# A hybrid diffusion trunk on one core: adaLN chunks moved between stages, a residual's split reordered, one more unnormed tile, an early chunk one pass later

## The chip, the core and the metric

The kernel runs on one core of a Trainium2 chip, as one program for the whole inference step. The metric is the device time of one execution in microseconds (us). A core's engines each work through their own queue in the order in which the program was written: TensorE (PE, with its weight loads as PEld), VectorE (DVE), ScalarE (ACT), GpSimd (POOL, next to idle here) and SyncE (SP, which issues the DMAs). They wait for each other through semaphores.

## The reference

Four layers on 384 tokens of width 1024 (128 context tokens, 256 latent tokens). The token mixer of layer i has kind i mod 3, and a ConvFFN follows each:

```python
for i in range(DEPTH):                       # 4
    kind, j = i % 3, i // 3
    sh1, sc1, gt1, sh2, sc2, gt2 = ada_params(cond, w_ada[i], b_ada[i])   # silu(cond) @ w_ada + b
    h = rms_norm(x, g_mix[i]) * (1 + sc1) + sh1
    if kind == 0:   y = chunk_gmlp(h, ...)   # u, v = split(gelu(h @ w_in)); (u * spatial(rms_norm(v))) @ w_out
    elif kind == 1: y = multi_pool(h, ...)   # centred mean over 2, 4, 8, 16 tokens minus h, grouped product
    else:           y = attention(h, ...)    # windowed, grouped queries, sinks
    x = x + gt1 * y
    h = rms_norm(x, g_ffn[i]) * (1 + sc2) + sh2
    a, u = split(h @ w_ffn_in[i])
    x = x + gt2 * ((gelu(depthwise_conv3(a)) * u) @ w_ffn_out[i])
```

All is float32. Outputs: x of both token groups, and the new keys and values.

## The kernel before, in words

x lies transposed in SBUF as 8 row tiles d = 0 to 7 of 128 x 384 (features on partitions, tokens along the row; 0 to 127 have the context's adaLN values, 128 to 383 the latent's, hence two column ranges, GRPS).

**Products.** A float32 product is made of three passes in fp32r: each operand is split into hi and lo, and wh\*rh + wl\*rh + wh\*rl are summed in PSUM (`mm3`, L688). Weights come in chunks of 128 x 1024 floats (512 KB) in one fixed order, `chunk_plan`. SP loads them into five buffers (`load`, L330); `w_split` has ACT copy a chunk to whi (L349) and DVE subtract to wlo (L356), some chunks ahead of PE (`w_get`).

**adaLN.** The 6 x 8 column groups of `w_ada` of each layer are chunks in the same stream, placed by the table ADA into stages ("gu", "go", "fi", "fo"; `weave` spreads them among a stage's weight chunks). An "ad" chunk is two DVE products with a sum (`ada_dve`, L391), taken in the stream's order behind the split of the weight chunk ahead of it. An "ap" chunk is four small matmuls (`ada_pe`, L409). The first two groups of layer 0 are "a0" chunks, on PE too (`a0_mm`, L1550; `a0_fin`, L1564).

**Residual and the next stage's input.** `out_proj` makes the eight d in five steps m: pairs (0,1), (2,3), (4,5), then 6 and 7 alone. After a step, `residual` updates x of each d on DVE (L464, two ranges), and `after(d)` of `prep` makes the *unnormed* input of the next stage, x times the gain A, split: on ACT hi = A\*x, two ranges (L624), on DVE lo = A\*x - hi, two ranges (L626), on ACT the square of x (L477), on DVE its sum (L479). For the pool's output `second` does the x update (L1057). Ahead of the pool, `extra` adds a bias to x on ACT (L1655). The ffn's `add_square` (L484) adds the last square, and `stats` (L536) then sums over features on PE.

**ffn.** Two column tiles (f = 0, 1) and those below NR = 3 are computed from the unnormed input and normed afterwards, with tile-wise products (L714, L719); meanwhile `norming` makes the normed input (`put_one`, L585 to L598), which the other 19 tiles of 22 use. "fr" and "fi" name chunks of the ffn's first product, "fo" of its second, "go" of the gMLP's output, "o" of the attention's. Stage names below are with the layer: go0, fo0, fi1, fo1.

**Start.** Layer 0's first product goes through k = 0 to 7 in `vmm` (three passes p of 6 matmuls); behind pass 0 `hook(k)` finishes the adaLN of k + 1 and has PE do the a0 chunks of k + 2.

## Time and profile before

| | |
|---|---|
| median of 3 runs | 1789.51 us (1787.81 to 1791.0) |
| the profiled execution | 1788.39 us, span 1786.6 us |
| granted TensorE clock, mean | 0.996 |
| PE busy | 1754.6 us (98%), 10230 matmuls |
| PEld busy | 1675.2 us (94%) |
| DVE busy | 1371.8 us (77%), 2369 instructions |
| ACT busy | 872.2 us (49%), 1635 instructions |
| weight DMAs, share of the 16 DMA engines | 50.9%, HBM 173 GB/s |
| chain that ended last, by engine | PE 61%, DVE 22%, ACT 8%, issue 5%, DMA 4% |

PE's busy share says little, since matmuls are pipelined and their ends modelled: what counts are the few places where PE waits, and who ends those waits. DVE's 77% is a mean over stages, some of which it fills.

### The profile page before, as it was taken

The numbers are of one execution on the slowest core, as the hardware profiler recorded it, in microseconds if no ns is written. First come the engines' busy times: TensorE is split into PE (matmuls) and PEld (weight loads), VectorE is DVE, ScalarE is ACT, GpSimd is POOL, SyncE is SP. The second block draws the span as 40 slices with busy tenths as digits, with TensorE's granted clock in tenths as the row PEclk, the third lists the DMA queues.
The fourth block names the chain that finished last, engine by engine and source line by source line (L and its number), as shares of the span: only waits on it lengthen the run. The fifth ranks groups of instructions, "written<-read, shape, count | busy, mean of one in ns | idle before, by whom it ended". The sixth has DMA issues, their size and how long they took to land.

```text
span 1786.6 us, 26835 instructions
## 1 busy us (share of the span) xinstructions
PE 1754.6 (98%) x10230; PEld 1675.2 (94%) x10230; DVE 1371.8 (77%) x2369; ACT 872.2 (49%) x1635; POOL 1.8 (0%) x30
## 2 busy tenths in 40 slices
PE   9999989999999999999998999999999999999999
PEld 7799889999998899998777999999988999999999
DVE  5888688888986888899687788887775767876632
ACT  3644236545455654432469565453454434755521
POOL 0000000000000000000000000000000000000000
PEclk9999999999999999999999999999999999999999
DMA  8764663555663355567550335655546344354341
GB/s 323 280 222 147 234 211 130 189 191 198 219 212 106 126 181 200 200 214 241 203 183 1 131 130 188 197 176 202 193 150 204 112 145 145 123 175 151 136 150 57
DMA packets 87636, 311.64 MB, mean 174 GB/s; under 512 B 10450, under 2 KB 10962, under 8 KB 87252
## 3 DMA queue, kind: packets, MB, share of 16 engines
q1 hardware_dynamic: 87220, 309.92, 50.9%
q8 instruction: 80, 1.31, 0.3%
q14 instruction: 48, 0.39, 0.1%
q10 hardware_dynamic: 288, 0.01, 0.0%
HBM read 308.06 MB, written 1.84 MB: 173 GB/s over the span
## 4 chain that ended last, share of the span: by engine, by line
PE 61%; DVE 22%; ACT 8%; issue 5%; DMA 4%; SPq 0%; DVEq 0%; ACTq 0%
PE mm L688 45%; DVE wlo L356 7%; DVE junk L391 7%; PE mm L862 6%; DMA wraw<-wts 4%; ACT whi L349 3%; DVE ct L736 3%; PE S L688 1%; PE mm L906 1%; ACT gg L745 1%; DVE gl L606 1%; PE adaT L688 1%; PE S L1138 1%; PE adaT L862 1%; PE psa L862 1%
## 5 line engine op out<-in xcount | busy, mean ns | idle before, releaser
L688 PE MATMUL mm<-hb,whi 128*128 128x384 f32 (+1 forms) x4064 | 888.7, 338 | 6.6 <-ACT whi L349 2.6
L688 PEld LDWEIGHTS mm<-hb,whi 128*128 128x128 f32 x4064 | 722.7, 189 | 11.6 <-ACT whi L349 3.3
L356 DVE TENSOR_TENSOR wlo<-wraw,whi 128x1024 fp32r<-128x1024 f32 (+2 forms) x390 | 466.3, 1201 | 213.7 <-ACT whi L349 212.4
L349 ACT ACTIVATE whi<-wraw 128x1024 fp32r<-128x1024 f32 (+2 forms) x390 | 399.3, 1034 | 270.3 <-PE mm L688 139.4
L688 PE MATMUL mm<-hb,wlo 128*128 128x384 f32 (+1 forms) x2032 | 521.4, 337 | 0.8 <-DVE wlo L356 0.8
L391 DVE SCALAR_TENSOR_TENSOR junk<-wraw,condb 128x1024 bf16<-128x1024 f32 x304 | 371.6, 1222 | 9.1 <-ACT condb L1618 2.7
L688 PEld LDWEIGHTS mm<-hb,wlo 128*128 128x128 f32 x2032 | 369.1, 189 | 1.3 <-DVE wlo L356 1.3
L745 ACT ACTIVATE gg<-ct 128x128 f32<-128x128 f32 (+1 forms) x152 | 47.0, 357 | 248.9 <-DVE ct L736 248.9
L688 PE MATMUL mm<-gh,whi 128*128 128x384 f32 x448 | 123.9, 338 | 3.2 <-ACT whi L349 3.2
L688 PE MATMUL mm<-gh,wlo 128*128 128x384 f32 x448 | 124.2, 338 | 2.4 <-DVE wlo L356 2.4
L688 PE MATMUL mm<-gl,whi 128*128 128x384 f32 x448 | 123.8, 338 | 0.0
L736 DVE SCALAR_TENSOR_TENSOR ct<-ab,par,ct 128x385 f32<-128x385 f32 x176 | 108.7, 619 | 6.4 <-ACT ct L734 2.7
L624 ACT ACTIVATE hb<-x,A 128x128 fp32r<-128x128 f32 x96 | 43.2, 457 | 103.9 <-DVE x L464 93.1
L862 PE MATMUL mm<-whi,hb 128*128 128x512 f32 x320 | 87.6, 399 | 0.0
L688 PEld LDWEIGHTS mm<-gh,whi 128*128 128x128 f32 x448 | 81.9, 189 | 4.1 <-ACT whi L349 4.1
L688 PEld LDWEIGHTS mm<-gh,wlo 128*128 128x128 f32 x448 | 82.0, 189 | 3.6 <-DVE wlo L356 3.6
L688 PEld LDWEIGHTS mm<-gl,whi 128*128 128x128 f32 x448 | 82.3, 189 | 0.0
L746 DVE TENSOR_TENSOR gg<-mm,gg 128x384 f32<-128x384 f32 x76 | 42.4, 558 | 47.4 <-ACT gg L745 46.7
L862 PEld LDWEIGHTS mm<-whi,hb 128*128 128x128 f32 x320 | 60.8, 190 | 15.6 <-ACT hb L573 0.4
L734 ACT ACTIVATE ct<-ab,par 128x385 f32<-128x385 f32 x88 | 62.7, 713 | 3.4
L464 DVE SCALAR_TENSOR_TENSOR x<-mm,prm,x 128x128 f32<-128x128 f32 x92 | 33.6, 411 | 22.9 <-PE mm L688 22.7
L862 PE MATMUL mm<-wlo,hb 128*128 128x512 f32 x160 | 47.8, 405 | 0.0
(286 smaller groups left out, 1651.8 us busy)
## 6 DMA issues: line engine op xcount, KB each, us to landing
wraw<-wts SPq DMA_DIRECT2D x562, 512.0 KB, 3.9
wraw<-wts SPq DMA_DIRECT2D x12, 256.0 KB, 2.6
wraw<-wts SPq DMA_DIRECT2D x8, 384.0 KB, 4.1
x<-x SPq DMA_DIRECT2D x4, 384.0 KB, 4.5
mx<-mix SPq DMA_DIRECT2D x1, 1280.0 KB, 7.8
y<-x SPq DMA_DIRECT2D x3, 384.0 KB, 3.1
condb<-condb SPq DMA_DIRECT2D x1, 1024.0 KB, 7.1
ws<-a_w_s SPq DMA_DIRECT2D x2, 512.0 KB, 4.3
```

Of the source, the lines that this page charges most:

```text
L349: nc.scalar.activation(hi[:, :n], t[:, :n], AF.Copy)
L356: nc.vector.tensor_tensor(out=lo[:, :n], in0=t[:, :n], in1=hi[:, :n].bitcast(F32), op=ALU.subtract)
L391: nc.vector.scalar_tensor_tensor(out=self.junk.bitcast(BF16), in0=w, scalar=1.0, in1=self.condb[:, c, :], op0=ALU.mult, op1=ALU.mult, accu ...
L464: nc.vector.scalar_tensor_tensor(out=x[:, d, t0:t1], in0=ps[:, t0:t1], scalar=self.prm[:, l, ty * 8 + d, c:c + 1], in1=x[:, d, t0:t1], op0 ...
L606: nc.vector.tensor_tensor(out=lo, in0=src, in1=hi.bitcast(F32), op=ALU.subtract)
L624: nc.scalar.activation(self.hh[:, d, t0:t1], self.x[:, d, t0:t1], AF.Copy, scale=A[:, d, c:c + 1])
L688: nc.tensor.matmul(o, w[:, c:c + nw], r, start=(first and p == 0), stop=(last and p == 2))
L734: nc.scalar.activation(t, ab[:, 1:T + 2], AF.Identity, scale=cw[1], bias=cb)
L736: nc.vector.scalar_tensor_tensor(out=t, in0=ab[:, i:i + T + 1], scalar=cw[i], in1=t, op0=ALU.mult, op1=ALU.add)
L745: nc.scalar.activation(g[:, t0:t1], t[:, t0 + c:t1 + c], GELU)
L746: nc.vector.tensor_tensor(out=g, in0=u, in1=g, op=ALU.mult)
L862: nc.tensor.matmul(ps[n][i], hs, w[p == 1][:, c:c + 512], start=(k == 0 and p == 0), stop=(k == 7 and p == 2))
```

## The change

Five edits. (1) The ADA table gives each stage another number of "ad" chunks: gu0 10 to 12, go0 12 to 8, fi0 18 as before, fo0 16 to 18, fi1 18 to 20, fo1 22 to 20. (2) In `after(d)` the square comes first. (3) A\*x is first written to a float32 tile xt (two ACT instructions), hi is an ACT copy of xt, and lo is one DVE subtraction over all 384 columns. (4) In the layer behind the pool, four ffn tiles are unnormed instead of three. (5) At the start, the a0 matmuls of k + 2 (and what hung on them) move from behind pass 0 to behind pass 1.

```diff
@@ -46,12 +46,12 @@
 
 ADA = {
     (0, "gv"): [("ad", 0, 4)],
-    (0, "gu"): [("ad", 0, 2), ("ad", 0, 3, 0, 2)],
-    (0, "go"): [("ad", 0, 3, 2, 8), ("ad", 0, 5, 0, 6), ("ap", 1, 1)],
-    (0, "fi"): [("ad", 0, 5, 6, 8), ("ad", 1, 2), ("ad", 1, 0)],
-    (0, "fo"): [("ad", 1, 4), ("ad", 1, 3)],
-    (1, "fi"): [("ad", 1, 5), ("ad", 2, 1), ("ad", 2, 0, 0, 2)],
-    (1, "fo"): [("ad", 2, 0, 2, 8), ("ad", 2, 4), ("ad", 2, 3)],
+    (0, "gu"): [("ad", 0, 2), ("ad", 0, 3, 0, 4)],
+    (0, "go"): [("ad", 0, 3, 4, 8), ("ad", 0, 5, 0, 4), ("ap", 1, 1)],
+    (0, "fi"): [("ad", 0, 5, 4, 8), ("ad", 1, 2), ("ad", 1, 0, 0, 6)],
+    (0, "fo"): [("ad", 1, 0, 6, 8), ("ad", 1, 4), ("ad", 1, 3)],
+    (1, "fi"): [("ad", 1, 5), ("ad", 2, 1), ("ad", 2, 0, 0, 4)],
+    (1, "fo"): [("ad", 2, 0, 4, 8), ("ad", 2, 4), ("ad", 2, 3)],
     (2, "nm"): [("ap", 2, 2, 0, 6)],
     (2, "qkv"): [("ap", 2, 2, 6, 8)],
     (2, "at"): [("ap", 2, 5)],
@@ -620,13 +620,13 @@
                 nc.vector.tensor_copy(self.hh[:, :, T:TE], sh)
                 nc.vector.tensor_tensor(out=self.hl[:, :, T:TE], in0=sh, in1=self.hh[:, :, T:TE].bitcast(F32),
                                         op=ALU.subtract)
+            res["sq"] = self.square(d, res["acc"])
+            t = self.tmp.tile([128, T], F32, tag="gg", name="xt")
             for c, (t0, t1) in enumerate(GRPS):
-                nc.scalar.activation(self.hh[:, d, t0:t1], self.x[:, d, t0:t1], AF.Copy, scale=A[:, d, c:c + 1])
-            for c, (t0, t1) in enumerate(GRPS):
-                nc.vector.scalar_tensor_tensor(out=self.hl[:, d, t0:t1], in0=self.x[:, d, t0:t1],
-                                               scalar=A[:, d, c:c + 1], in1=self.hh[:, d, t0:t1].bitcast(F32),
-                                               op0=ALU.mult, op1=ALU.subtract)
-            res["sq"] = self.square(d, res["acc"])
+                nc.scalar.activation(t[:, t0:t1], self.x[:, d, t0:t1], AF.Copy, scale=A[:, d, c:c + 1])
+            nc.scalar.activation(self.hh[:, d, 0:T], t, AF.Copy)
+            nc.vector.tensor_tensor(out=self.hl[:, d, 0:T], in0=t, in1=self.hh[:, d, 0:T].bitcast(F32),
+                                    op=ALU.subtract)
             if extra is not None:
                 extra(d)
 
@@ -688,7 +688,7 @@
                 nc.tensor.matmul(o, w[:, c:c + nw], r, start=(first and p == 0), stop=(last and p == 2))
 
 
-    def ffn(self, l, pr, follow, stat_k):
+    def ffn(self, l, pr, follow, stat_k, nr):
 
 
         nc = self.nc
@@ -708,7 +708,7 @@
             pos = ((1, TC + 1), (TC + 2, T + 2))
 
             def epi_a(f, pa, pu):
-                if f >= NR:
+                if f >= nr:
                     return f, pa, None, pu, None
                 a1 = self.tmp.tile([128, T], F32, tag="sq", name="a1")
                 nc.vector.tensor_tensor(out=a1, in0=pa[:, 0:T], in1=rbs, op=ALU.mult)
@@ -802,11 +802,11 @@
                         w = self.w_get("fi")
                         for st, g in zip(sts, gs):
                             self.split_act(g, gh[st[0]], gl[st[0]])
-                    if f < NR:
+                    if f < nr:
                         norm(3)
                     for k4 in range(4):
                         k = 4 * kk + k4
-                        r = (hh[:, k, :], hl[:, k, :]) if f < NR else (nh[:, k, :], nl[:, k, :])
+                        r = (hh[:, k, :], hl[:, k, :]) if f < nr else (nh[:, k, :], nl[:, k, :])
                         self.mm3([(pa, 256 * k4), (pu, 256 * k4 + 128)], w, r, k == 0, k == 7)
                 prev.append((f, pa, pu))
             assert next(steps, 0) == 0 and len(prev) == 1
@@ -861,8 +861,8 @@
                             hs = (vl if p == 2 else vh)[:, k, 128 * i:128 * i + 128]
                             nc.tensor.matmul(ps[n][i], hs, w[p == 1][:, c:c + 512],
                                              start=(k == 0 and p == 0), stop=(k == 7 and p == 2))
-                    if p == 0 and hook is not None and len(cs) == 2:
-                        hook(k)
+                    if p < 2 and hook is not None and len(cs) == 2:
+                        hook[p](k)
 
             def vout(b, ps):
                 for i in range(3):
@@ -1605,10 +1605,12 @@
         a0_mm(1)
         nc.sync.dma_start(self.cst[:, 0:512], a["cst"][:, 0:512])
 
-        def hook(k):
+        def hook0(k):
             if k + 1 < KD:
                 a0_put(k + 1, a0_fin(k + 1))
-                a0_mm(k + 2)
+
+        def hook1(k):
+            a0_mm(k + 2)
             if k == 3:
                 nc.sync.dma_start(self.condb, a["condb"].rearrange("p (c d) -> p c d", c=2))
             if k == 7:
@@ -1623,7 +1625,7 @@
             kind, j = l % 3, l // 3
             prep = lambda l=l: self.prep(l, 1)
             if l == 0:
-                pr = self.gmlp(l, j, prep, None, hook)
+                pr = self.gmlp(l, j, prep, None, (hook0, hook1))
             elif kind == 0:
                 pr = self.gmlp(l, j, prep, pr)
             elif kind == 1:
@@ -1657,7 +1659,7 @@
 
                 return self.prep(l + 1, 0, bias)
 
-            pr = self.ffn(l, pr, follow, 4 if kind == 1 else 2)
+            pr = self.ffn(l, pr, follow, *((4, NR + 1) if kind == 1 else (2, NR)))
         self.mm_ctx.close()
```

Three more hunks only replace `f >= NR` or `f < NR` by `f >= nr` or `f < nr` (L729, L743, L792), so that nr reaches all places where the ffn tells unnormed tiles from normed ones.

**Order on PE at the start**, first product of layer 0, the piece of the difference for k = 0 (hb is the input's split, psa the a0 chunks' sums, L1564 their transposes, L862 the product's passes):

```order
 L1564 MATMUL a0T<-cst,a0row 128x2 x2
+L862 MATMUL mm<-wlo,hb_83 128x512 x6
 L1550 MATMUL psa<-wraw,cond 32x256 x8
-L862 MATMUL mm<-wlo,hb_83 128x512 x6
 L862 MATMUL mm<-whi,hb_83 128x512 x12
```

The wlo pass of six matmuls now stands ahead of the eight a0 matmuls of k + 2, which were ahead of it; the same holds for the later k.

**Order on DVE in fo0**, the residual of the second pair, d = 2 and 3. Before:

```order
L464 SCALAR_TENSOR_TENSOR x<-mm,prm,x 128x128
L464 SCALAR_TENSOR_TENSOR x<-mm,prm,x 128x256
L626 SCALAR_TENSOR_TENSOR hb_84<-x,A,hb_84 128x128
L626 SCALAR_TENSOR_TENSOR hb_84<-x,A,hb_84 128x256
L479 TENSOR_TENSOR acc<-acc,sq 128x384
```

and now:

```order
L464 SCALAR_TENSOR_TENSOR x<-mm,prm,x 128x128
L464 SCALAR_TENSOR_TENSOR x<-mm,prm,x 128x256
L479 TENSOR_TENSOR acc<-acc,sq 128x384
L628 TENSOR_TENSOR hb_84<-xt,hb_84 128x384
```

acc now stands ahead of lo, and lo (into hb_84) is one instruction that reads xt and hi. In both, the same rows follow for d = 3, so x of d = 3 stands behind lo of d = 2. **ACT, same place.** Before:

```order
L624 ACTIVATE hb_84<-x,A 128x128
L624 ACTIVATE hb_84<-x,A 128x256
L477 ACTIVATE sq<-x 128x384
L1655 ACTIVATE x<-x,pgb 128x128
L1655 ACTIVATE x<-x,pgb 128x256
```

and now:

```order
L477 ACTIVATE sq<-x 128x384
L626 ACTIVATE xt<-x,A 128x128
L626 ACTIVATE xt<-x,A 128x256
L627 ACTIVATE hb_84<-xt 128x384
L1657 ACTIVATE x<-x,pgb 128x128
L1657 ACTIVATE x<-x,pgb 128x256
```

hi has moved from the first two of five instructions to the fourth of six. Behind the pair, ACT goes on with whi of the next weight chunks.

**Order on DVE at the start of fo0**, up to x of d = 0 (L391 rows are ad chunks, wlo rows weight chunks). Before:

```order
L356 TENSOR_TENSOR wlo<-wraw,whi 128x1024 x2
L391 SCALAR_TENSOR_TENSOR junk,prm<-wraw,condb 128x1024 x2
L356 TENSOR_TENSOR wlo<-wraw,whi 128x512
L391 SCALAR_TENSOR_TENSOR junk,prm<-wraw,condb 128x1024 x2
L356 TENSOR_TENSOR wlo<-wraw,whi 128x1024
L391 SCALAR_TENSOR_TENSOR junk,prm<-wraw,condb 128x1024 x2
L356 TENSOR_TENSOR wlo<-wraw,whi 128x1024 x2
L391 SCALAR_TENSOR_TENSOR junk,prm<-wraw,condb 128x1024 x2
L464 SCALAR_TENSOR_TENSOR x<-mm,prm,x 128x128
```

and now:

```order
L356 TENSOR_TENSOR wlo<-wraw,whi 128x1024
L391 SCALAR_TENSOR_TENSOR junk,prm<-wraw,condb 128x1024 x2
L356 TENSOR_TENSOR wlo<-wraw,whi 128x1024
L391 SCALAR_TENSOR_TENSOR junk,prm<-wraw,condb 128x1024 x2
L356 TENSOR_TENSOR wlo<-wraw,whi 128x512
L356 TENSOR_TENSOR wlo<-wraw,whi 128x1024
L391 SCALAR_TENSOR_TENSOR junk,prm<-wraw,condb 128x1024 x2
L356 TENSOR_TENSOR wlo<-wraw,whi 128x1024
L391 SCALAR_TENSOR_TENSOR junk,prm<-wraw,condb 128x1024 x2
L356 TENSOR_TENSOR wlo<-wraw,whi 128x1024
L391 SCALAR_TENSOR_TENSOR junk,prm<-wraw,condb 128x1024 x2
L464 SCALAR_TENSOR_TENSOR x<-mm,prm,x 128x128
```

Five ad chunks (x2 each) stand ahead of x of d = 0 instead of four. Between the first and the second pair it is five instead of four again, between the second and the third five in both, behind that one in both.

## Rows read from the trace of the kernel before

**Rows 1.** Chain that ended last; start, us, engine, line, instructions: products of ffn 2.

```profile
1025.92 270.83 PE mm L688 x1560
```

**Rows 2.** Timeline of PE (start, us, line, out<-in, count, idle before and releaser): its waits.

```profile
246.17 0.44 PE L688 MATMUL mm<-hb,whi 128*128 128x384 f32 x1 [2.58 <-ACT whi L349]
...
260.84 0.80 PE L536 MATMUL cs<-ones,acc 128*128 128x1 f32 x6 [2.09 <-DVE acc L484]
...
523.05 0.45 PE L688 MATMUL mm<-gh,wlo 128*128 128x384 f32 x1 [0.31 <-DVE wlo L356]
...
600.13 0.98 PE L688 MATMUL mm<-hb,whi 128*128 128x384 f32 x4 [2.26 <-DVE hb L589]
```

**Rows 3.** Windows: the start, the end of go0, and fi1 with fo1.

```profile
core 0: us, PE busy (x) PEld busy (x) DVE busy (x) ACT busy (x) POOL busy (x), PEclk, DMA share, GB/s
20.50:25.00 4.50, 4.50 (x20) 3.40 (x13) 1.95 (x3) 1.06 (x1) 0.00 (x0) 0.62 1.04 407
246.20:253.60 7.40, 6.58 (x20) 6.33 (x21) 7.30 (x12) 0.86 (x1) 0.00 (x0) 0.54 0.45 151
...
600.00:842.00 242.00, 235.66 (x1335) 232.65 (x1335) 213.93 (x328) 106.18 (x196) 0.00 (x0) 0.99 0.61 204
```

**Rows 4.** Timeline of DVE in fo0: the residual of the second pair.

```profile
491.75 0.74 DVE L464 SCALAR_TENSOR_TENSOR x<-mm,prm,x 128x128 f32<-128x128 f32 x2
...
493.48 0.56 DVE L479 TENSOR_TENSOR acc<-acc,sq 128x384 f32<-128x384 f32 x1
493.96 0.74 DVE L464 SCALAR_TENSOR_TENSOR x<-mm,prm,x 128x128 f32<-128x128 f32 x2
...
497.48 1.23 DVE L356 TENSOR_TENSOR wlo<-wraw,whi 128x1024 fp32r<-128x1024 f32 x1 [1.23 <-ACT whi L349]
```

**Rows 5.** Timeline of ACT: the same pair, and a copy in layer 1's norm.

```profile
492.13 0.90 ACT L624 ACTIVATE hb<-x,A 128x128 fp32r<-128x128 f32 x2 [1.57 <-DVE x L464]
492.94 0.51 ACT L477 ACTIVATE sq<-x 128x384 f32<-128x384 f32 x1
...
496.40 2.51 ACT L349 ACTIVATE whi<-wraw 128x1024 fp32r<-128x1024 f32 x3
...
581.47 0.53 ACT L588 ACTIVATE hb<-nt 128x384 fp32r<-128x384 f32 x1
```

**Rows 6.** Timeline of PE at the start: a0 matmuls of k = 2, a later wlo pass.

```profile
20.15 0.64 PE L1550 MATMUL psa<-wraw,cond 128*32 128x256 f32 x8 [1.73 <-DMA wraw<-wts]
...
28.00 1.66 PE L862 MATMUL mm<-wlo,hb 128*128 128x512 f32 x6
```

**Rows 7.** Page, costliest groups: the instructions of the ad chunks.

```profile
L391 DVE SCALAR_TENSOR_TENSOR junk<-wraw,condb 128x1024 bf16<-128x1024 f32 x304 | 371.6, 1222 | 9.1 <-ACT condb L1618 2.7
```

**Rows 8.** Timeline of DVE: a wait in go0, the split behind fo0's first pair.

```profile
215.55 1.22 DVE L356 TENSOR_TENSOR wlo<-wraw,whi 128x1024 fp32r<-128x1024 f32 x1 [5.54 <-ACT whi L349]
...
475.08 1.23 DVE L356 TENSOR_TENSOR wlo<-wraw,whi 128x1024 fp32r<-128x1024 f32 x1 [1.23 <-ACT whi L349]
```

**Rows 9.** Timeline of PE in fo0: the passes that use those two splits.

```profile
478.03 0.51 PE L688 MATMUL mm<-gh,wlo 128*128 128x384 f32 x2
...
500.91 0.51 PE L688 MATMUL mm<-gh,wlo 128*128 128x384 f32 x2
```

**Rows 10.** Timelines of DVE and PE behind the pool: last sum of squares, statistics.

```profile
567.32 0.56 DVE L484 TENSOR_TENSOR acc<-acc,sq 128x384 f32<-128x384 f32 x1
...
572.53 0.72 PE L536 MATMUL cs<-ones,acc 128*128 128x1 f32 x6
```

**Rows 11.** Timelines of DVE and PE at the attention's output, layer 2.

```profile
999.49 0.74 DVE L464 SCALAR_TENSOR_TENSOR x<-S,prm,x 128x128 f32<-128x128 f32 x2 [1.55 <-PE S L688]
...
1007.81 0.74 DVE L464 SCALAR_TENSOR_TENSOR x<-S,prm,x 128x128 f32<-128x128 f32 x2 [1.06 <-PE S L688]
...
1019.39 0.56 DVE L484 TENSOR_TENSOR acc<-acc,sq 128x384 f32<-128x384 f32 x1
...
1020.19 0.72 PE L536 MATMUL cs<-ones,acc 128*128 128x1 f32 x6
```

More of the change, by code (lines that the diff above doesn't have):

```diff
@@ L742, in epi_c @@
                 g = self.tmp.tile([128, T], F32, tag="gg", name="gg")
-                if f >= NR:
+                if f >= nr:
                     for c, (t0, t1) in enumerate(GRPS):
@@ L791, in ffn @@
             for f in range(2, NF):
-                w0 = TE if f < NR else T
+                w0 = TE if f < nr else T
                 pa, pu = self.bank()[:, :w0], self.bank()[:, :w0]
@@ L804, in ffn @@
                             self.split_act(g, gh[st[0]], gl[st[0]])
-                    if f < NR:
+                    if f < nr:
                         norm(3)
```

## The prediction, made before the change was run

> **What bounds the kernel now.** I read the chain that ended last first, to get PE's pace: 1560 products in 270.83 us, 0.1736 us each [rows 1]. TensorE's clock is at its upper level, 2.4 GHz, almost throughout, so the time is PE's pace plus the places where PE waits. Those come from PE's timeline [rows 2]: at 246.17 for a weight's hi half, at 260.84 for the sum of squares ahead of layer 0's statistics, at 523.05 for a lo half, at 600.13 for a lo half of the normed input. Each of these waits ends in DVE or in ACT, which waits in DVE's order. The windows [rows 3] then say two things. In two short stretches, at the start and at the end of go0, the granted clock was 0.62 and 0.54, the latter near 1.2 GHz, each right behind a wait of PE. And from 600 to 842 (fi1, fo1) PE idled 6.3 us while DVE was busy 213.9 of 242: there DVE paces. In fo0 PE waited only 0.31 us, so what DVE gets to do there more shows almost at once. 0.2% of this kernel, 3.6 us, is about what a measurement can tell from no change.
>
> **The residual's new split** is what most terms hang on. DVE's timeline [rows 4]: from x of d = 2 to x of d = 3 is 493.96 - 491.75 = 2.21 us: x, lo, acc, without a wait. Lo needs no wait because ACT begins hi 0.38 us behind x's start, as soon as the first range is there [rows 4, 5]. In the new order x of d + 1 stands behind lo of d, and lo behind ACT's whole chain: square, two writes of xt, copy. Step by step: x 0.74, a hop of 0.04 (estimate: square's end 493.45 to acc's start 493.48 is 0.03), the square 0.42 (0.51 [rows 5], less the 0.09 by which ACT starts the next instruction ahead of the end: the pair at 492.13 is 0.90 long, the square starts 0.81 behind it), the xt pair 0.90, a hop 0.03, the copy 0.53 (the one at 581.47 has its shape), a hop 0.03, lo 0.48 (as acc, 493.48 to 493.96). That is 3.17: **+0.96 for each d**, +1.45 for the first pair, where d = 0 had no acc. The next weight chunk's hi comes later too: before, ACT took it up at 496.40, 2.44 behind the second x; now at 0.74 + 0.04 + 0.42 + 0.90 + 0.03 + 0.53 and some 0.6 for ACT's x pair (an estimate, less than its pair at 492.13) = 3.28, +0.84. So a pair puts DVE's next weight split back by 1.8, the first by about 2.0 (0.4 was idle there). Ends: by DVE's busy time alone the spacing would be 0.74 + 0.04 + 0.48 + 0.48 = 1.74, -0.47 each; with every hop and the square at full length 3.4, +1.2.
>
> The Trainium skill's page "Perfetto Trace Analysis", section "Optimizing Scalar/DVE Operations", holds that grouping into larger operations can improve throughput if the engine is saturated; and also, against this change, that where these engines aren't saturated but cause bubbles on others, "breaking up instructions may allow work to be completed sooner". The rows bear out the second: the hi in two slices is what lets lo start without a wait now. By the first the sum below would fall by some 22 us; it is a rival.
>
> **Start** (hook). PE waits 1.73 us for a weight at 20.15 [rows 6], and the clock in the 4.5 us behind it is 0.62 [rows 3], a loss of 4.5 x 0.38 = 1.7. The wlo pass (1.66 at full clock, 28.00) now goes ahead of the a0 matmuls and fills most of the wait: -1.5, and with PE not idle the clock loss too: **-3.2**. Ends -1.2 (a part of the wait alone) and -3.4. The adaLN of k + 2 comes one pass later; a pass of slack is left, since it is finished behind the next k's pass 0.
>
> **gu0, two more ad chunks**, 2 x 1.222 = 2.44 each [rows 7]: 4.9 of DVE, covered by DVE's idle there, of which the wait of 5.54 at 215.55 [rows 8], also fed by that stage's loads, is the largest piece: 0. If that cover is gone it is +2.
>
> **go0**, four fewer. Three go ahead of the first pair that ends late (-7.3), one behind (-2.4). Against it the two pairs ahead +3.8, and behind them one pair, one single d and the last +4.3 (1.8; 0.96 + 0.1; 1.45). The wait at 215.55 is for loads that ad chunks had delayed; taking half of it as gone is -2.9. Sum -4.5: statistics at 256.3 instead of 260.84. **-4.5**; PE's waits there (2.58 + 0.82 as it was followed up, 2.09) and the clock at 0.54 for 7.4 us (3.4) sum to about 9, the lower end; the upper is -1.7, with none of the 5.54 gone.
>
> **fo0**, two more. Five ad chunks stand ahead of the first residual instead of four, and five instead of four behind it. The weight split behind the first pair [rows 8] starts at 475.08; now +2.44 and +2.0: 479.5. It is done 1.23 later; the pass that uses it began at 478.03 [rows 9], so PE waits 480.8 - 478.0 = 2.75. Behind the second pair: 497.48 [rows 4] + 4.44 + 2.44 + 1.8, done by 507.5, for a pass at 500.91 + 2.75 [rows 9]: 3.8. Behind the third, with no more ad chunks, the wait at 523.05 [rows 2] comes 8.7 + 1.8 = 10.5 later on DVE, against 6.55 on PE: 4.0 more. Sum 10.5, less a half for short waits of DVE on the way: **+10**. Ends +3 (the lead that DVE has from fi0 larger than the rows show) and +12.
>
> **Pool.** Its d run on the same spacing. The last sum starts at 567.32, ends 0.56 later and is needed at 572.53 [rows 10], 4.6 of cover. Seven spacings by 0.96 and the last product's lo make 7.1, so the statistics come 2.7 late, and the later copies that PE's small products wait for add a little: **+3.5**. Ends +1 (two spacings hidden beside PE's products) and +5.
>
> **Fourth unnormed tile.** It takes away the wait at 600.13 (2.26). But DVE paces what follows [rows 3], so PE would only wait later, in fo1; what stays is DVE's two products for that tile, 2 x 0.56 (as rows 10's sum): **+1.2**. Ends -2.3 (the wait gone and no other for it) and +2. Two ad chunks go from fo1 to fi1, both stages that DVE paces: 0.
>
> **Attention's output, layer 2.** DVE waited 1.55 and 1.06 for PE ahead of x of d = 2 and 4, and the last sum ends at 1019.95, 0.24 before PE's statistics at 1020.19 [rows 11]: no cover. The first pair puts x of d = 2 back by 2.5 - 1.55 = 0.95, the second x of d = 4 by 0.95 + 1.8 + 0.1 - 1.06 = 1.8; from there 0.96 + 1.07 + 1.07 + 1.45 = 4.55 to the sum (1.07: a weight split behind a d where ACT has no x pair to do). 6.3 less 0.24: **+6.0**. Ends +3 and +6.5.
>
> **fo2, go3**: the same spacing, but hardly any ad chunks, and no wait of PE in the rows I read: 0, with DVE's idle as cover; +2 if it isn't there.
>
> **Sum**: -3.2 - 4.5 + 10 + 3.5 + 1.2 + 6.0 = +13.0. The profiled execution took 1788.39, which makes 1801.4; the median of the runs is 1.1 above it, so **1802.5**.
>
> **The rivals.** *Faster*: DVE does not wait on the copy, the spacing falls to 1.74 and not to 3.17. Then go0 gives all of 9.3, fo0 costs 2 (two chunks of 2.44, less 0.47 per d and 1.7 of slack), the pool and the attention nothing: -3.2 - 9.3 + 2 + 1.2, **1780**. Against it stands the order: lo of d ahead of x of d + 1, the copy behind three other ACT instructions. For it, that the hops and ACT's overlap are bounds of mine. Between 1.74 (-9.3) and 3.17 (+13) the sum crosses zero at a spacing of about 2.35, just above today's 2.21. This is what the skill's first rule would make of it. *No change*: go0 gives 9.3 and fo0's lead hides 3.5 of its 10, the pool and the attention cost 2.5 and 3: -3.2 - 9.3 + 6.5 + 2.5 + 1.2 + 3 = +0.7, **1790**. For it, that DVE has some lead over PE in fi0 that I can't read; against it, no row shows it. *Slower still*: behind the new waits of 4 to 6 us the clock falls as at 246.20 (0.54 for 7.4 us, 3.4 each [rows 3]); with the statistics of layer 2 and one place in fo0 +6, **1808**. For it, that both low stretches of the rows follow a wait; against it, that the wait of 2.26 at 600.13 left the window's clock at 0.99.
>
> **How the numbers follow.** My forecast 0.51, slower still 0.20, no change 0.11, faster 0.18. The range holds the forecast's own bounds and slower still up to 1811, and reaches down into no change; of the faster rival it takes in the half that lies nearest: 1784 to 1811. The forecast's own range is 1792 to 1808. Faster by over 0.2%: the faster rival, 0.18; within 0.2%: no change, 0.10; slower: the rest, 0.72.
>
> **What would show it.** On DVE's timeline the spacing of two x of a pair in fo0: 3.2 means the main term is right, below 2.4 wrong. PE's waits behind each pair in fo0 near 3 to 4 us; statistics of layer 0 some 4 us earlier than the start's gain alone makes them; no wait of PE at 20 and none at layer 1's fifth tile, but more in fo1; the statistics of layer 2 waiting 6 us for the sum. Wrong would be: no wait in fo0 although the spacing is 3.2 (DVE's lead was larger), or a spacing that stays at 2.2.

## The result, and the profile after

The changed kernel took 1805.63 us (median of 4 runs, 1804.6 to 1808.77) against 1789.63 in the runs of the kernel before beside it: ratio 1.0093, interval 1.0076 to 1.011. It is slower, some 16 us. Some executions, of the kernel before too, take 20 to 70 us longer than the others; ratios and medians leave them out.

| | before | after |
|---|---|---|
| profiled execution, us | 1788.39 | 1806.07 |
| span, us | 1786.6 | 1804.3 |
| PE busy | 1754.6 (98%) | 1763.4 (98%) |
| DVE busy | 1371.8 (77%) | 1359.7 (75%) |
| ACT busy | 872.2 (49%) | 891.9 (49%) |

DVE has 12 us less to do, ACT 20 more, and the kernel is slower. Where that comes from is read from the residual first. DVE's timeline of the changed kernel, second pair of fo0 (start, us, line, count, idle before and releaser), answers to [rows 4]:

```profile
494.73 0.74 DVE L464 SCALAR_TENSOR_TENSOR x<-mm,prm,x 128x128 f32<-128x128 f32 x2
496.06 0.56 DVE L479 TENSOR_TENSOR acc<-acc,sq 128x384 f32<-128x384 f32 x1 [0.59 <-ACT sq L477]
497.31 0.56 DVE L628 TENSOR_TENSOR hb<-xt,hb 128x384 fp32r<-128x384 f32 x1 [0.69 <-ACT hb L627]
497.79 0.74 DVE L464 SCALAR_TENSOR_TENSOR x<-mm,prm,x 128x128 f32<-128x128 f32 x2
...
502.01 1.22 DVE L356 TENSOR_TENSOR wlo<-wraw,whi 128x1024 fp32r<-128x1024 f32 x1 [1.08 <-ACT whi L349]
```

Two waits, 0.59 for the square and 0.69 for the copy, stand where there was none. From x to x it is 3.06 us instead of 2.21, and from the pair's first x to the next weight's split 502.01 - 494.73 = 7.28 instead of 497.48 - 491.75 = 5.73. ACT's timeline of the same place answers to [rows 5]:

```profile
495.50 0.53 ACT L477 ACTIVATE sq<-x 128x384 f32<-128x384 f32 x1 [4.36 <-DVE x L464]
495.93 0.79 ACT L626 ACTIVATE xt<-x,A 128x128 f32<-128x128 f32 x2
496.75 0.53 ACT L627 ACTIVATE hb<-xt 128x384 fp32r<-128x384 f32 x1
...
500.94 2.51 ACT L349 ACTIVATE whi<-wraw 128x1024 fp32r<-128x1024 f32 x3
```

ACT begins only when all of x is there (0.77 behind its start; before, 0.38), and takes four instructions to the copy. The square's 0.53 costs 0.43 up to the next start. PE's timeline of the changed kernel, its longer waits, answers to [rows 2]:

```profile
255.31 0.81 PE L536 MATMUL cs<-ones,acc 128*128 128x1 f32 x6 [4.52 <-DVE acc L484]
...
475.63 0.62 PE L688 MATMUL mm<-gh,whi 128*128 128x384 f32 x2 [1.99 <-ACT whi L349]
476.90 0.62 PE L688 MATMUL mm<-gh,wlo 128*128 128x384 f32 x2 [0.64 <-DVE wlo L356]
502.03 0.62 PE L688 MATMUL mm<-gh,whi 128*128 128x384 f32 x2 [0.75 <-ACT whi L349]
503.29 0.62 PE L688 MATMUL mm<-gh,wlo 128*128 128x384 f32 x2 [0.64 <-DVE wlo L356]
527.38 0.44 PE L688 MATMUL mm<-gh,whi 128*128 128x384 f32 x1 [2.32 <-ACT whi L349]
528.64 0.44 PE L688 MATMUL mm<-gh,wlo 128*128 128x384 f32 x1 [0.82 <-DVE wlo L356]
...
609.63 0.45 PE L688 MATMUL mm<-hb,whi 128*128 128x384 f32 x1 [1.69 <-ACT be L717]
...
850.83 0.45 PE L688 MATMUL mm<-gh,whi 128*128 128x384 f32 x1 [1.54 <-ACT whi L349]
852.08 0.44 PE L688 MATMUL mm<-gh,wlo 128*128 128x384 f32 x1 [0.81 <-DVE wlo L356]
...
1028.73 0.94 PE L688 MATMUL mm<-hb,whi 128*128 128x386 f32 x4 [1.41 <-DVE x L464]
1036.27 0.80 PE L536 MATMUL cs<-ones,acc 128*128 128x1 f32 x6 [3.05 <-DVE acc L484]
```

The six rows from 475.63 to 528.64 are the waits behind the three pairs of fo0, 7.16 us where the row at 523.05 was the only one. The windows behind the waits answer to [rows 3] (columns as there; PEclk is the first number behind the five engines):

```profile
core 0: us, PE busy (x) PEld busy (x) DVE busy (x) ACT busy (x) POOL busy (x), PEclk, DMA share, GB/s
255.30:262.00 6.70, 6.69 (x31) 6.70 (x32) 3.43 (x8) 0.90 (x2) 0.00 (x0) 0.75 0.46 159
475.60:481.00 5.40, 4.73 (x17) 4.40 (x18) 5.35 (x7) 2.29 (x3) 0.00 (x0) 0.71 0.41 142
...
527.30:535.00 7.70, 6.80 (x28) 6.55 (x29) 6.98 (x11) 2.82 (x6) 0.00 (x0) 0.78 0.52 177
609.60:615.00 5.40, 5.07 (x19) 4.83 (x20) 5.18 (x8) 1.53 (x4) 0.00 (x0) 0.68 0.34 108
851.00:857.00 6.00, 5.19 (x20) 4.93 (x21) 5.93 (x10) 1.46 (x2) 0.00 (x0) 0.72 0.48 170
1036.20:1042.00 5.80, 5.73 (x26) 5.76 (x27) 3.49 (x8) 0.95 (x2) 0.00 (x0) 0.71 0.54 173
```

In six places the granted clock fell behind waits, each a loss of 1.6 to 1.7 (5.4 x 0.29 = 1.6, 7.7 x 0.22 = 1.7): behind 4.52 us, 2.63 (1.99 + 0.64), 3.14, 1.99 (1.69 and a following 0.30), 2.35 and 3.05. In the kernel before it fell in three, the two low ones of [rows 3] and one in fo1, behind waits of 1.07 and 0.64:

```profile
766.00:773.00 7.00, 5.29 (x20) 4.65 (x19) 6.06 (x8) 4.39 (x6) 0.00 (x0) 0.76 0.34 112
```

None of these three is left; at the end of go0 the clock is 1.00 from 241 to 250. All in all the clock takes some 10 us now (six times 1.7) and took 6.8 before (1.7, 3.4 and 1.7).

How the difference grows is seen from PE's own instructions. Both executions have 10230 matmuls, in the same order but for the start; the table takes the start of the same matmul in a kernel and in the kernel before, and gives the difference (us; negative is earlier). The columns are times in the kernel before: behind the start, behind the go0 statistics, at the begin and end of fo0, in fi1 behind the norm, at fi1's end, behind fo1, ahead of and behind the attention's statistics, at the end.

```text
kernel                     54    290    460    532    612    750    845   1010   1045   1782
after                    -2.6   -3.9   -4.2    7.2    8.7   13.1   11.0   11.2   17.7   17.6
e1_old_split             -1.9   -9.7   -9.9   -4.9   -4.4    0.0   -3.5   -1.7   -1.7   -1.7
e2_split_only            -1.8    7.2    7.1   14.6   17.2   17.2   17.0   17.1   23.5   23.7
e3_ada_only              -1.9  -10.0  -10.2   -6.3   -6.3   -2.7   -4.4   -4.4   -4.4   -4.4
e4_hook_nr               -3.0   -2.9   -3.0   -3.4   -2.9   -2.8   -0.8   -0.7   -0.7   -0.7
e5_square_last           -2.6   -8.3   -8.5   -0.6    0.3    4.8    1.4    1.4    3.8    3.7
e6_two_slices            -2.7   -7.2   -7.4   -0.4   -0.1    4.5    2.4    2.4    4.2    4.2
e7_lo_one_later          -2.8   -4.8   -5.0    3.3    3.3    8.3    6.3    6.2    8.8    8.8
e12_idle_copy_again      -2.7   -6.4   -6.7    1.3    1.2    6.2    4.0    3.9    4.7    4.7
e8_start_and_layer0      -2.8  -10.5  -10.7   -6.1   -6.1   -6.2   -6.2   -6.3   -6.3   -6.3
e9_two_in_fi0            -3.0  -11.4   -6.7   -7.3   -7.3   -7.3   -7.3   -7.3   -7.3   -7.3
e11_two_in_gu0           -2.8   -8.7   -8.7   -9.3   -9.0   -9.3   -7.5   -7.1   -7.1   -7.1
```

By it the change gave 2.6 at the start and 1.3 in go0, and lost 11.4 in fo0, 1.5 behind the pool, 2.3 in fi1 and fo1, 6.5 at the attention's output. Executions of one kernel differ (27 of the kernel before, run beside the first experiments, took 1785.27 to 1793.04 us), and a fall of the clock, 1.7 us, comes in one and not in another, so the table serves for stages, and the medians for totals.

### The profile page after: what moved, and what is told of

Its sections match the earlier page's. It is cut to its first block, busy times and chain, and to the rows that moved or that the text cites. A ratio compares the mean times of both kernels' runs of the same rounds, so it can differ in the third digit from the quotient of the medians.

```text
span 1804.3 us, 26833 instructions
## 1 busy us (share of the span) xinstructions
PE 1763.4 (98%) x10230; PEld 1678.8 (93%) x10230; DVE 1359.7 (75%) x2324; ACT 891.9 (49%) x1684; POOL 1.8 (0%) x30
## 4 chain that ended last, share of the span: by engine, by line
PE 60%; DVE 23%; ACT 9%; issue 5%; DMA 3%; DVEq 0%; ACTq 0%
PE mm L688 45%; DVE wlo L356 7%; DVE junk L391 7%; PE mm L862 6%; ACT whi L349 3%; DVE ct L736 3%; DMA wraw<-wts 3%; PE mm L906 1%; DVE x L464 1%; ACT gg L745 1%; ACT xt L626 1%; DVE gl L606 1%; PE S L1138 1%; PE adaT L862 1%; PE psa L862 1%
## 5 line engine op out<-in xcount | busy, mean ns | idle before, releaser
L391 DVE SCALAR_TENSOR_TENSOR junk<-wraw,condb 128x1024 bf16<-128x1024 f32 x304 | 371.4, 1222 | 9.2 <-ACT condb L1620 2.7
L477 ACT ACTIVATE sq<-x 128x384 f32<-128x384 f32 x49 | 25.7, 525 | 125.0 <-DVE x L464 116.1
L862 PE MATMUL mm<-whi,hb 128*128 128x512 f32 x320 | 87.3, 398 | 0.2 <-ACT hb L573 0.2
L862 PEld LDWEIGHTS mm<-whi,hb 128*128 128x128 f32 x320 | 59.4, 187 | 17.5 <-issue 2.5
L628 DVE TENSOR_TENSOR hb<-xt,hb 128x384 fp32r<-128x384 f32 x48 | 26.8, 559 | 47.0 <-ACT hb L627 47.0
```

Source lines behind the costliest of these rows:

```text
L391: nc.vector.scalar_tensor_tensor(out=self.junk.bitcast(BF16), in0=w, scalar=1.0, in1=self.condb[:, c, :], op0=ALU.mult, op1=ALU.mult, accu ...
L477: nc.scalar.activation(sq, self.x[:, d, :], AF.Square)
L628: nc.vector.tensor_tensor(out=self.hl[:, d, 0:T], in0=t, in1=self.hh[:, d, 0:T].bitcast(F32), op=ALU.subtract)
L862: nc.tensor.matmul(ps[n][i], hs, w[p == 1][:, c:c + 512], start=(k == 0 and p == 0), stop=(k == 7 and p == 2))
```

## The experiments

The changes were tried apart first. Theory S: the residual's new split costs the time, because DVE stands in its order behind ACT's chain. Rival A: the two ad chunks more in fo0 and in fi1 cost it.

**e1_old_split.** The changed kernel with the old lines in `after(d)`:

```diff
-            res["sq"] = self.square(d, res["acc"])
-            t = self.tmp.tile([128, T], F32, tag="gg", name="xt")
...
+            for c, (t0, t1) in enumerate(GRPS):
+                nc.scalar.activation(self.hh[:, d, t0:t1], self.x[:, d, t0:t1], AF.Copy, scale=A[:, d, c:c + 1])
...
+            res["sq"] = self.square(d, res["acc"])
```

Expected: 

> The changed kernel with the residual's split as before (hi in two slices first, lo in two, square last); ADA table, fourth tile and start as changed. Theory S (the split's chain on ACT, for which DVE waits in its order, costs the time): spacing of two x of a pair in fo0 2.2 us instead of 3.06, no wait of PE for the sum at the attention's output, fo0's three waits shrink from about 8 us to 3, go0 gives 8: about 1784 us, some 5 below the kernel before. Rival A (the two ad chunks more in fo0 and in fi1 cost it, the split is nearly free): about 1803 us, fo0's waits stay.

Measured: 1784.77 us, ratio to before 0.9983 (0.9974 to 0.9992): 3 us faster than before, and 20.9 faster than the changed kernel by the medians, 1.1% by the ratios. The whole loss is in the split, and the other three edits together gain a little. DVE's timeline of this kernel at the second pair of fo0 shows the old rhythm back:

```profile
487.38 0.74 DVE L464 SCALAR_TENSOR_TENSOR x<-mm,prm,x 128x128 f32<-128x128 f32 x2
488.19 0.98 DVE L626 SCALAR_TENSOR_TENSOR hb<-x,A,hb 128x128 fp32r<-128x128 f32 x2
489.10 0.56 DVE L479 TENSOR_TENSOR acc<-acc,sq 128x384 f32<-128x384 f32 x1
489.58 0.74 DVE L464 SCALAR_TENSOR_TENSOR x<-mm,prm,x 128x128 f32<-128x128 f32 x2
...
493.09 1.22 DVE L356 TENSOR_TENSOR wlo<-wraw,whi 128x1024 fp32r<-128x1024 f32 x1 [1.23 <-ACT whi L349]
```

Spacing 2.20, first x to the next split 5.71.

**e2_split_only.** The kernel before with the changed lines of `after(d)` alone, the diff's third hunk. Expected: 

> The kernel before with only the residual's split changed (square first, xt, copy, one lo). Theory S: go0's end +5 to +8 us, fo0 +5, pool +1, attention's output +6: about 1809 us. Rival A: no more than +3, about 1792 us.

Measured: 1811.56 us, ratio 1.0122 (1.0107 to 1.0138): +22 us by the ratio. By the table go0 loses 9.0, fo0 7.5, pool 2.6, the attention 6.4. In go0 PE's timeline of this kernel shows the old waits of [rows 2] doubled:

```profile
248.40 0.69 PE L688 MATMUL mm<-hb,whi 128*128 128x384 f32 x1 [4.66 <-ACT whi L349]
...
265.24 1.41 PE L536 MATMUL cs<-ones,acc 128*128 128x1 f32 x6 [5.01 <-DVE acc L484]
```

and its windows show the clock at half, 1.2 GHz, behind both:

```profile
248.00:254.00 6.00, 5.03 (x15) 4.63 (x16) 5.51 (x8) 1.30 (x2) 0.00 (x0) 0.50 0.39 132
...
265.00:271.00 6.00, 5.76 (x20) 5.79 (x21) 3.66 (x9) 1.13 (x2) 0.00 (x0) 0.50 0.57 189
```

Rival A falls.

**e3_ada_only.** The kernel before with only the ADA lines. Expected: 

> The kernel before with only the new ADA table. Theory S: go0 -8, fo0 +3 (two ad chunks of 2.44 against some slack), fi1 and fo1 +2: about 1786.5 us. Rival A: the loss of the whole change is here, about 1804 us.

Measured: 1785.65 us, ratio 0.9989 (0.998 to 0.9998). By the table: go0 -8.1, fo0 +3.9, fi1 +3.6, fo1 -1.7. The two ad chunks of 2.44 that fo0 gained cost it 3.9, nearly all of their 4.9. The two that went from fo1 to fi1 cost 1.9 on balance in this execution: fi1 paid 3.6, fo1 gave back 1.7. What fo1 gave back is uncertain by the clock, which fell there once in either execution, at 769 before and in e3 at 837 (0.57 from 837 to 841), 1.7 us each; e1, with the same table, has no fall there (1.00 from 837.6 to 843).

**e4_hook_nr.** The kernel before with the start's a0 products one pass later and `*((4, NR + 1) if kind == 1 else (2, NR))`. Expected: 

> The kernel before with only the start's a0 products one pass later and the fourth unnormed tile. Both theories: PE 2.7 us earlier from 54 us on; the wait of 2.3 at layer 1's fourth tile gone. If DVE paces fi1 and fo1, the tile gives nothing back or costs 1.2: 1787 to 1788.5 us; if not, it gives 2.3 more: 1784.7 us.

Measured: 1788.10 us, ratio 0.9996 (0.9987 to 1.0005): nothing. PE's timeline shows what became of the wait at 600.13 [rows 2]:

```profile
598.04 0.44 PE L688 MATMUL mm<-hb,whi 128*128 128x384 f32 x1 [2.02 <-ACT be L717]
598.78 0.66 PE L688 MATMUL mm<-hb,whi 128*128 128x384 f32 x1 [0.31 <-DVE u L719]
```

It is nearly as long as before and now for the fourth tile's own arithmetic. By the table 2.1 are lost in fo1 besides, but the clock fell more there than in the kernel before (0.57 from 765 to 773 and from 841 to 845, 3.4 and 1.7, against 1.7), so this execution does not price the tile. The fourth tile gives nothing.

Then the split was taken apart. Rival L: only the square's place at the head costs. Rival W: ACT's added instruction delays the weights' hi halves.

**e5_square_last.** The changed kernel, the line with `self.square` moved behind lo. Expected: 

> The changed kernel with the square last again (xt, xt, copy, square on ACT; lo, sum on DVE). Theory S: the next x still stands behind lo and the sum, lo now waits 0.78 + 0.90 + 0.03 + 0.53 = 2.24 and the sum follows: spacing 2.24 + 2 x 0.5 = 3.2, so no better than the changed kernel, 1804 to 1808 us. Rival L (the square's place at the head of ACT's queue is what costs): spacing back near 2.3, about 1786 us.

Measured: 1795.44 us, ratio 1.0044 (1.0029 to 1.006). The expectation under S missed: the spacing is 2.82, not 3.2, because the first write of xt starts as soon as x's first range is there, which I had left out (the old hi does the same). Rival L would be 1786. DVE's timeline:

```profile
489.05 0.74 DVE L464 SCALAR_TENSOR_TENSOR x<-mm,prm,x 128x128 f32<-128x128 f32 x2
...
491.87 0.74 DVE L464 SCALAR_TENSOR_TENSOR x<-mm,prm,x 128x128 f32<-128x128 f32 x2
...
495.93 1.23 DVE L356 TENSOR_TENSOR wlo<-wraw,whi 128x1024 fp32r<-128x1024 f32 x1 [1.17 <-ACT whi L349]
```

**e6_two_slices.** The square first, then the old four lines for hi and lo. Expected: 

> The changed kernel with the square first, but hi and lo in two slices straight from x, as before (no xt, no copy). Theory S: lo's first slice can start 0.78 + 0.04 + 0.42 + 0.45 = 1.7 behind x, both slices and the sum are done at 2.7: spacing 2.65, half way from 2.2 to 3.06, so about half of the 21 us that the split costs: 1794 to 1796 us. Rival L (the square's place alone): as the changed kernel, 1805 us; if the xt detour alone costs: 1785 us.

Measured: 1793.92 us, ratio 1.0039 (1.0024 to 1.0053), at the lower edge of what was expected; the spacing is 2.47, a little less than expected, first x to split 6.54. DVE's timeline:

```profile
490.20 0.74 DVE L464 SCALAR_TENSOR_TENSOR x<-mm,prm,x 128x128 f32<-128x128 f32 x2
492.67 0.74 DVE L464 SCALAR_TENSOR_TENSOR x<-mm,prm,x 128x128 f32<-128x128 f32 x2
...
496.74 1.23 DVE L356 TENSOR_TENSOR wlo<-wraw,whi 128x1024 fp32r<-128x1024 f32 x1 [1.52 <-ACT whi L349]
```

With e1 and the changed kernel e5 and e6 make a square of four: neither edit 1784.8, the square first alone +9.1, the detour over xt alone +10.7, both +20.9 (by the ratios 10.0, 10.9 and 19.7). The two edits of the split cost about the same, and nearly add.

**e7_lo_one_later.** The changed kernel with the subtraction held back by one d:

```diff
+            if "lo" in res:
+                res.pop("lo")()
             res["sq"] = self.square(d, res["acc"])
...
+            if d < KD - 1:
+                res["lo"] = lo
+            else:
+                lo()
```

Expected: 

> The changed kernel with lo of d issued behind x of d + 1 (for the last d at once): the same instructions, only DVE no longer stands in line behind the copy before the next x. Theory S (DVE's order, not the work): ACT's chain of some 2.4 us becomes the spacing; fo0's waits and the attention's shrink to less than half: 1788 to 1795 us. Rival W (the added ACT work, one instruction of 0.53 a d, is what delays the weights' hi): no change, 1803 to 1806 us.

Measured: 1796.34 us, ratio 1.0048 (1.0031 to 1.0066), just above S's range and below W's. DVE's order costs something, but not all. DVE's timeline:

```profile
492.23 0.74 DVE L464 SCALAR_TENSOR_TENSOR x<-mm,prm,x 128x128 f32<-128x128 f32 x2
...
494.04 0.73 DVE L464 SCALAR_TENSOR_TENSOR x<-mm,prm,x 128x128 f32<-128x128 f32 x2
...
498.81 1.22 DVE L356 TENSOR_TENSOR wlo<-wraw,whi 128x1024 fp32r<-128x1024 f32 x1 [2.33 <-ACT whi L349]
```

Its spacing is 1.81, below that of the kernel before, and yet the next split comes 6.58 behind the first x, because it waits 2.33 us for ACT, which is still at the pair. So S had to be widened to theory C: what PE feels is the time from the pair's first x to the next weight's split, whichever engine makes it.

**e10_idle_copy, e12_idle_copy_again.** To tell C from S: the old split, with an ACT instruction that nobody reads.

```diff
             res["sq"] = self.square(d, res["acc"])
+            t = self.tmp.tile([128, T], F32, tag="gg", name="xt")
+            nc.scalar.activation(t, self.x[:, d, :], AF.Copy)
```

Expected: 

> The changed kernel with the old split, and behind each square one more ACT copy of 128 x 384 that nobody reads: ACT gets the change's added instruction (0.43 to 0.53 a d) while DVE's order and work are the old ones. Theory C (formed after the last runs: what PE feels is the time from a pair's first x to the next weight's split, through DVE and ACT alike): that time grows from 5.71 to some 6.4, the spacing of two x hardly; 1790 to 1793 us, where the old split without the copy took 1784.8. Theory S alone (only DVE's wait between two x costs): 1785 us.

Measured: ratio 1.0018 (1.0007 to 1.0028), its median 1792.34. The profile below is of a second run of the same kernel. Expected: 

> The kernel with the old split and one idle ACT copy a d once more, for a profile without the slow matmuls that the first one had in its later half. Theory C: spacing of two x 2.20, first x to the next weight's split 6.3 in fo0, PE some 2 us later by the end of fo0 and 4 to 6 in all than in the old split without the copy: 1789 to 1792 us. Theory S alone: 1785 us.

Measured: 1789.41 us, ratio 1.0009 (0.9999 to 1.0018). The ratios lie above e1's 0.9983 by 0.35% and 0.26%, some 5 to 6 us for an instruction with no reader and a DVE that has exactly the work that it had. DVE's timeline of the second run:

```profile
490.81 0.74 DVE L464 SCALAR_TENSOR_TENSOR x<-mm,prm,x 128x128 f32<-128x128 f32 x2
493.02 0.73 DVE L464 SCALAR_TENSOR_TENSOR x<-mm,prm,x 128x128 f32<-128x128 f32 x2
497.10 1.23 DVE L356 TENSOR_TENSOR wlo<-wraw,whi 128x1024 fp32r<-128x1024 f32 x1 [1.64 <-ACT whi L349]
```

The spacing is 2.21, the split 6.29 behind the first x. That is theory C, and not S alone. It is also rival W's mechanism: the added ACT instruction does delay the hi halves, but by e7 and the square of four that is a part, 5 to 6 us of some 20. The six kernels with the changed ADA table, start and fourth tile, side by side:

```text
kernel                  x to x   first x to next split   median us
e1_old_split             2.20          5.71               1784.8
e12_idle_copy_again      2.21          6.29               1789.4 (1792.3 in e10)
e6_two_slices            2.47          6.54               1793.9
e7_lo_one_later          1.81          6.58               1796.3
e5_square_last           2.82          6.88               1795.4
after                    3.06          7.28               1805.6
```

The time follows the second column in its order; the first alone puts e7 in the wrong place. e7 and e5 stand too near each other to be told apart. The column gives no price: 1.17 from e1 to e5 go with 10.7 us, 0.40 from e5 to the changed kernel with 10.2. By the table the traces differ in that last step by 4.4 in go0, 3.5 in fo0 and 4.1 at the attention's output. In go0 and at the attention PE waits for the sum ahead of the statistics, which one pair of fo0 doesn't show: 2.49 and 2.06 in e5, with the clock at 1.00 behind both, 4.52 and 3.05 in the changed kernel, with a fall behind each.

Last, versions without the split and the fourth tile.

**e8_start_and_layer0.** The old split, `(2, NR)` and `(4, NR)` as before, the new table for layer 0 only. Expected: 

> The kernel before with the start's a0 products one pass later and layer 0's part of the new ADA table (gu0 12, go0 8, fi0 18, fo0 18); split, three unnormed tiles and layer 1's ad chunks as before. Theory S and the single runs: start -1.5, go0 -9, fo0 +3.5, nothing behind: about 1780.5 us. If fi1 and fo1 fill up again whatever comes early (DVE paces them from their own start): 1784 us, as the changed kernel with the old split.

Measured: 1784.26 us, ratio 0.9977 (0.9967 to 0.9988), above the 1780.5 expected; its profiled execution was 1782.14. The time is what the rival reading gave, that DVE in fi1 and fo1 eats what comes early, but by the table nothing is lost any more there, so that reading fell; fo0 still loses 4.6. e8 and e1 differ only by the fourth tile and layer 1's table: ratios 0.9977 and 0.9983, with intervals that overlap, so these two edits together cost 1 us or nothing.

**e9_two_in_fi0, e11_two_in_gu0.** e8 with fo0's two ad chunks elsewhere:

```diff
-    (0, "fi"): [("ad", 0, 5, 4, 8), ("ad", 1, 2), ("ad", 1, 0, 0, 6)],
-    (0, "fo"): [("ad", 1, 0, 6, 8), ("ad", 1, 4), ("ad", 1, 3)],
+    (0, "fi"): [("ad", 0, 5, 4, 8), ("ad", 1, 2), ("ad", 1, 0)],
+    (0, "fo"): [("ad", 1, 4), ("ad", 1, 3)],
```

for e9, and for e11 the lines become

```diff
+    (0, "gu"): [("ad", 0, 2), ("ad", 0, 3, 0, 6)],
+    (0, "go"): [("ad", 0, 3, 6, 8), ("ad", 0, 5, 0, 6), ("ap", 1, 1)],
+    (0, "fi"): [("ad", 0, 5, 6, 8), ("ad", 1, 2), ("ad", 1, 0)],
+    (0, "fo"): [("ad", 1, 4), ("ad", 1, 3)],
```

Expected of e9: 

> As the kernel with the start and layer 0's table, but the two ad chunks that fo0 gained put into fi0 instead (gu0 12, go0 8, fi0 20, fo0 16). If fo0 is where DVE has no slack and fi0 has some (DVE busy 21.5 of 25 us there): fo0 as before, no wait, 3 to 4 us below that kernel, 1781 us. If fi0 has none, as fi1 behind the pool had none: the same 1785 us, with waits in fi0.

Expected of e11: 

> The same two ad chunks put into gu0 instead (gu0 14, go0 8, fi0 18, fo0 16). If gu0 still has idle DVE after the first two more: 1781 us. If its slack is used up: waits ahead of go0, 1784 to 1786 us.

Measured: e9 1783.21 us, ratio 0.9979 (0.9965 to 0.9993); e11 1780.09 us, ratio 0.9957 (0.9944 to 0.9971). In e9 the loss only moves: the table has it lose 4.7 between 290 and 460, in fi0, whose slack I had read from DVE's busy share. In e11 the stage gu0 loses 3.1 (-2.8 at 54, +0.3 at 240; e8 0.6), of which go0 takes up some: behind it e11 stands 1.8 behind e8 (-8.7 and -10.5); and fo0 loses nothing. e11 is faster than both kernels of this study, by 0.43% against the one before; its interval touches e8's, so that it beats e8 is likely, not shown.

## Why the prediction was right

The forecast was 1802.5 (1784 to 1811), slower, and 1805.6 came. The mechanism was right: DVE stands in its order behind ACT's longer chain, and PE behind DVE's later splits. Some of the sizes agree by luck, and that is said below. Point by point, against the changed kernel's trace:

- **The residual's split**, the main term, was right by its own steps: the spacing 3.17 was 3.06, and the second x to the next split 3.52 + 0.84 = 4.36 was 502.01 - 497.79 = 4.22. The 0.1 too much is the 0.90 of the xt pair: it takes 0.79 when x is already there. The prediction had both parts of theory C (DVE's line and ACT's lateness), added; the first expectations of the experiments had dropped the second, and e7 and e12 brought it back.
- **fo0**, +10 forecast, +11.4 measured, by the steps named. The split behind the first pair was put at 479.5, behind the second at 506.2; with PE 4.2 ahead on entering, the trace has them at 475.62 + 4.2 and 502.01 + 4.2. The waits were 2.6, 1.4 and 3.1 and not 2.75, 3.8 and 4.0: behind the first and the third the clock fell and took 1.6 and 1.7. What PE lost behind the first pair by the clock made it come later to the second, where it waited less; the last loss came on top. So DVE's lateness was right, but the waits sum to 7.2 where 10.5 was forecast, and that the total is near is in part luck: the clock, which the term left out, makes up the difference. Of the 11.4, two ad chunks are 3.9 to 4.6 (e3, e8) and the split 7.5 (e2).
- **Attention's output**, +6.0 forecast, +6.5 measured: waits of 1.41 and 3.05 and 1.7 of clock. Here too the size agrees by luck: the statistics were to wait 6 us and waited 3.05, and the clock wasn't in the term.
- **go0** failed in size: -4.5 forecast, -1.3 measured. The ADA table gave its 8 (e3) but the split took 9 alone (e2). The statistics came at 255.31 instead of 260.84, 5.5 earlier, of which 2.6 are the start's: go0 gave 2.9 there. The forecast took half of DVE's wait of 5.54 [rows 8] as gone and put that at 2.9, but only 0.8 of it went (the row at 209.74 below). Then the statistics waited 4.52 us for the sum, and the clock fell behind that (0.75 for 6.7 us, 1.7 lost), which the term didn't have.
- **Pool**, +3.5 forecast, +1.5 measured; alone (e2) 2.6, of which 1.7 is the clock (0.66 from 578 to 583). The statistics, put 2.7 late, had no wait at all (580.68, in the place of 572.53). In the kernel before DVE waited there for PE ahead of x, and the first spacings went into that wait, which the step did not count (the row at 553.64 below). What PE lost in the pool is one wait of 0.95 for DVE's copy of u.
- **Fourth tile**, +1.2 forecast, and **two ad chunks from fo1 to fi1**, 0: together 2.3 in the trace from 612 to 845, but by the ratios of e1 and e8 1 us or nothing, so the forecast is within what can be told. Rightly nothing was put down for the wait that goes, but not for the reason given: another wait took its place at once, 1.69 us for the tile's own arithmetic (in e4 2.02), and not in fo1. The chunks alone cost 1.9 in e3's execution: fi1 had no slack behind the pool's layer and paid 3.6, and what fo1 gives back is uncertain by a fall of the clock.
- **Start**, -3.2 forecast, -2.6 in the trace, but this is right only in part. The kernel before was at a clock of 0.79 from 18 to 26 us in its profiled execution; e2 and e3, with the same start, were at 1.00 and 1.8 and 1.9 earlier at 54 us. e3 even had PE's wait there, 1.62, without a fall. So the clock part (1.7) belonged to that execution and not to its code; the kernels with the edit are 1.9 (e1) to 3.0 (e4) earlier at 54, so the edit itself gives about 1, or nothing in e1.
- Of the rivals, *slower still* held half: the clock fell in six places, but for 1.7 each where 3.4 was put down, and the three old low stretches were gone, 3.4 more in all. The 0.99 from 600 to 842 that was held against it is the fall in fo1 at 769; behind 600.13 itself the clock stayed at 1.00 (600.1 to 606). *No change* needed go0 to give 9.3, and it gave 1.3. *Faster*, with a spacing of 1.74, was refuted by the spacing, and e7, which has 1.81, is still slower than before: the break-even at a spacing of 2.35 was worked out from the wrong quantity.

The two rows on DVE's timeline, go0 in the changed kernel and the pool in the kernel before:

```profile
209.74 1.23 DVE L356 TENSOR_TENSOR wlo<-wraw,whi 128x1024 fp32r<-128x1024 f32 x1 [4.72 <-ACT whi L349]
...
553.64 0.74 DVE L1057 SCALAR_TENSOR_TENSOR x<-mm,pgs,x 128x128 f32<-128x128 f32 x2 [1.73 <-PE mm L1054]
```

The sum was 13.0 and the trace gives 17.6 (+16 by the medians). Of the 4.6 that are missing go0 is 3.2, half of it the clock. The sum had the clock at 1.7 less (the start), and by the count above it came to 3.4 more; the waits themselves, taken together, were forecast a little too long.

On the Trainium skill's page "Perfetto Trace Analysis", section "Optimizing Scalar/DVE Operations": its advice to group operations is for an engine that is saturated, and in fo0 DVE nearly is (before, busy 70.06 of the 78 us from 453 to 531); yet the grouped lo, with which DVE is busy 15 us less in all (1357.4 against 1372.6), cost 10.7 us on this path (e5 against e1), because its input had to be grouped too, on another engine and ahead of it. The other sentence, that breaking up instructions may let work be completed sooner, agrees with this case, though the page says it of engines that aren't saturated: the sliced hi begins 0.38 us behind x.

## What to carry to other kernels

Where an engine works in order, price an instruction by when the next engine can go on and not by its length: 0.5 us of ACT a d, in front of a weight's split, cost 5 to 6 us, even with no reader (e10, e12). Measure from the event that starts the burst to the first work that PE needs behind it (a weight's split, or the sum ahead of the statistics), over all engines in the line; the busy time of one of them, or its spacing, can fall while that grows (e7). And slack read from a busy share isn't slack: fi0, with DVE at 86%, paid 4.7 of the 4.9 us of two more chunks (e9).

## What was not expected of the hardware

The granted clock fell behind short waits of PE, and not behind each: in the changed kernel behind 1.7 to 4.5 us, to 0.68 to 0.78 over the next 5 to 8 us, each time for a loss of 1.6 to 1.7; in e2, behind 4.66 and 5.01 us, to 0.50 over 6 us, 3 us each. Behind the second pair of fo0, with 1.4 us of waits, it stayed at 1.00 in the window of the six us that follow. The length of the wait alone does not tell: the wait of 2.26 us for the normed input's lo half left it at 1.00 in the kernel before (600.1 to 606) and is followed by 0.62 in e3, where the same wait is just as long:

```profile
593.79 0.96 PE L688 MATMUL mm<-hb,whi 128*128 128x384 f32 x4 [2.26 <-DVE hb L589]
594.50:599.00 4.50, 4.50 (x19) 4.27 (x18) 4.16 (x6) 1.99 (x6) 0.00 (x0) 0.62 0.24 73
```

The same start of the program ran at 0.79 in the kernel before and at 1.00 in e2 and e3, so a clock loss seen in one execution isn't a part of the code's price until a second one shows it.
